# Split activations and split weights placed 32 bytes further into a 256-byte line, tile by tile

## The chip, the cores and the metric

The kernel runs on one core of a Trainium2 chip. Its time is device microseconds, the median of several runs. One execution is also recorded by the hardware profiler; times of single instructions come from that record.

## What is computed

A trunk of two layers on x, 512 tokens by 1024 features, in float32, with a norm behind it:

```
for i in range(DEPTH):                    # DEPTH = 2
    h = rmsnorm(x, norm_mix_g[i])
    h = chunked_spatial_gating(h, ...)    # layer 0: w_in [1024, 4096], w_out [2048, 1024]
    h = retention(h, ...)                 # layer 1 instead: w_in [1024, 6144], w_out [2048, 1024]
    x = x + h
    h = rmsnorm(x, norm_ffn_g[i])
    a = relu(h @ mlp_w1[i])               # [1024, 4096]
    x = x + (a * a) @ mlp_w2[i]           # [4096, 1024]
return rmsnorm(x, final_norm_g)
```

Nearly all of the arithmetic is in the products with the weight matrices.

## The kernel before, in words

**Three products for one.** A float32 product is made of float32r products, a faster and less exact form. Every operand is split into a high part (itself, rounded to float32r) and a low part (the rest). `mm3` (L207 to L210) adds high by high (L208), and the two mixed products (L209 and L210), into the same 128x512 block of PSUM; low by low is left out. A matmul here has 128x128 stationary weights, which PE loads ahead with an instruction of its own (PEld in the profile), and 512 moving columns.

**Activations.** The residual stream lies in xT: eight tiles xT0 to xT7 of 128 features by 512 tokens. `norm_split` (L219 to L223) makes of them hH0 to hH7 and hL0 to hL7, the split input of the products that follow a norm; these tiles are kept for the whole kernel. The results of the products lie in "big" tiles of 8192 bytes a partition, of which ten take turns: aH and aL (the squared activations of the dense layer), yH, yL, ryH and ryL (the mixers' gated results), q, k, v and others.

**Weights.** All matrices come in pieces of 1 MB by DMA into the tiles raw (two buffers of 8192 bytes). Each megabyte is two pieces. `prep` (L165 to L176) converts a piece into a tile wH (ScalarE, L172) and subtracts for wL (VectorE, L176); there are four buffers of wH and three of wL, of 4096 bytes each, taken in turn. `prep_tiles` (L160 to L163) takes the next buffers. The pieces have three shapes for three kinds of product, each with 1024 elements a partition: eight blocks of 128 columns, four of 256 or two of 512.

**Order.** The program is a list of steps written out by hand, each with one or two pieces of weights, and `refill` prepares the pieces ahead of the step that needs them. Evacuations and norms run behind later products. The names of products in the profile: v and u (gating's input), sg (its spatial mixing), o (its output); qk, vv and g (retention's input), sc and av (its scores and values), ro (its output); up and dn or dt (the two dense products, dt with tokens on the output's partitions, in the last layer). In v, u, qk, vv, g and up the activations are hH and hL; in o, ro, dn and dt they are slices of big tiles. In v, vv and dt the activations are the stationary operand and the weights the moving one, in the others it is the other way round.

**Where tiles lie.** Tiles are laid out in each partition in the order in which they are allocated, each rounded up to 32 bytes. The pool of kept tiles comes first: xT0 to xT7, hH0 to hH7, hL0 to hL7 (2048 bytes each), then ident, onesr and rows (512 each), gT (320), wide (4096), r4 and rh4 (16), vgh (64), rows2 (512), ssqv (64), rs4 (16), r2 (16), ssf (32) and ms0 (16), the last six at the places in the code where they are first needed. Behind it lie the weights' pool (two raw, four wH, three wL), the ten big tiles and the small working tiles. The first of the kept tiles begins 128 bytes into a 256-byte line.

Of the kernel before, what the change touches and what calls it, by code (L numbers as in the profile page):

```python
# [10 lines left out]
F32 = mybir.dt.float32  # L11
F32R = mybir.dt.float32r
# [5 lines left out]
P = 128  # L18
T = 512
D = 1024  # L20
KD = D // P
NT = T // P
# [10 lines left out]
class Raw:  # L33
    """A megabyte of a weight matrix as it lies in SBUF: [128, a, b]."""

# [4 lines left out]
class Piece:  # L40
    """Half of a Raw, split into two float32r parts."""

# [5 lines left out]
def pieces_f(w, rows, cols):  # L48
    """Stationary weights: pieces [128, 8 k, 128 columns]."""
    out = []  # L50
    for c in range(cols[0], cols[1], 256):
        raw = Raw(w[rows[0] : rows[1], c : c + 256].rearrange("(k p) n -> p k n", p=P))
        for i in range(2):
            out.append(Piece(raw, (slice(None), slice(None), slice(i * P, (i + 1) * P)), [P, 8, P]))
    return out


def pieces_t(w, rows, cols, parts=1):
    """Moving weights: pieces [128, 2 k, 512 columns]."""
    out = []  # L60
    for r in range(rows[0], rows[1], 512):
        raw = Raw(w[r : r + 512, cols[0] : cols[1]].rearrange("(k p) n -> p k n", p=P), parts)
        for i in range(2):
            out.append(Piece(raw, (slice(None), slice(2 * i, 2 * i + 2), slice(None)), [P, 2, 512]))
    return out


def pieces_o(w, rows, cols):
    """Stationary weights of 512 rows: pieces [128, 4 k, 256 columns]."""
    out = []  # L70
    for c in range(cols[0], cols[1], 512):
        raw = Raw(w[rows[0] : rows[1], c : c + 512].rearrange("(k p) n -> p k n", p=P))
        for i in range(2):
            out.append(Piece(raw, (slice(None), slice(None), slice(i * 256, (i + 1) * 256)), [P, 4, 256]))
    return out
# [3 lines left out]
def trunk(ctx, tc, x, norm_mix_g, norm_ffn_g, a_w_in, a_b_in, a_v_norm_g, a_w_s, a_b_s, a_w_out,  # L79
# [32 lines left out]

# [1 line left out]
    xT = [keep.tile([P, T], F32, name=f"xT{k}") for k in range(KD)]  # L114
    hH = [keep.tile([P, T], F32R, name=f"hH{k}") for k in range(KD)]
    hL = [keep.tile([P, T], F32R, name=f"hL{k}") for k in range(KD)]
    ident = keep.tile([P, P], F32, name="ident")
    onesr = keep.tile([P, P], F32R, name="onesr")
    rows = keep.tile([P, P], F32, name="rows")
    gT = keep.tile([P, 80], F32, name="gT")  # L120
    wide = keep.tile([P, D], F32, name="wide")
    rbc, r2bc = wide[:, 0:T], wide[:, T:D]
    r4 = keep.tile([P, NT], F32, name="r4")
    rh4 = keep.tile([P, NT], F32, name="rh4")
    vgh = keep.tile([P, 16], F32, name="vgh")
    make_identity(nc, ident)
    nc.gpsimd.memset(rows, 1.0)
# [7 lines left out]
    ]  # L135
    rows2 = keep.tile([16, P], F32, name="rows2")
    nc.scalar.dma_start(out=rows2, in_=vecs[0])
    nc.scalar.copy(out=onesr, in_=rows)
    MIX, FFN, VG, HG, BU = 0, 16, 32, 48, 64

# [1 line left out]
    order, steps, raws, pending = [], [], [], []  # L142
# [17 lines left out]
    def prep_tiles(i):  # L160
        p = order[i]
        p.hi = wts.tile(p.shape, F32R, tag="wH", name=f"wH{i}", bufs=4)
        p.lo = wts.tile(p.shape, F32R, tag="wL", name=f"wL{i}", bufs=3)  # L163

    def prep(upto, low=None):  # L165
        """Split the weights: the upper parts of all pieces before `upto`, the lower ones of those before `low`."""
        low = upto if low is None else low
# [38 lines left out]
    def mm3(ps, ah, al, bh, bl, start, stop):  # L206
        """ps += a.T @ b, of the parts' products all but the least."""  # L207
        nc.tensor.matmul(ps, lhsT=ah, rhs=bh, start=start, stop=False)  # L208
        nc.tensor.matmul(ps, lhsT=ah, rhs=bl, start=False, stop=False)  # L209
        nc.tensor.matmul(ps, lhsT=al, rhs=bh, start=False, stop=stop)  # L210

# [1 line left out]
    state = {}  # L213
# [5 lines left out]
    def norm_split(k, gcol):  # L219
        """h = x * g in two parts (the norm's scale comes in behind the product)."""  # L220
        g = gT[:, gcol + k : gcol + k + 1]
# [12 lines left out]
    def rsqrt(dst, a, n, name):  # L234
        """dst = a ** -0.5 on [128, n], by Newton's steps from the bits' half."""
        y, t = [work.tile([P, n], F32, tag=f"rs{i}_{n}", name=f"{name}_{i}", bufs=2) for i in range(2)]
# [22 lines left out]
    def stats(ssq, dst, scale, name):  # L259
        """dst[token, chunk] = rsqrt(mean of squares + eps)."""  # L260
        hi, lo = split(ssq, f"st_{name}", nc.gpsimd)
# [12 lines left out]
    def spread(src, dst, name):  # L274
        """dst[any partition, token] = src[token, chunk]."""
        d = []
# [10 lines left out]
    def norm(name, wide=True, square=False):  # L287
        """The statistics of the norm just summed, in steps behind work that doesn't need them."""
        yield from stats(state["ssq"], r4, 1.0 / D, name)
# [4 lines left out]

# [1 line left out]
    def mm_f(p, ps, bH, bL, ks, last):  # L296
# [8 lines left out]
    def feat(p, bufs, evac, name, behind=None):  # L305
        """One piece of stationary weights against all of b; behind() goes after the product."""
        def run(p):
# [9 lines left out]
    def feat_late(p, q, evacs, name):  # L317
        """Two pieces at once, each with the last k behind the others of both."""
        def run(p, q):
# [12 lines left out]
    def tokens(plist, bufs, evac, name, behind=None, last=None):  # L332
        """Pieces of moving weights: token-major results, four chunks at once."""
        accs = {}
# [29 lines left out]

# [1 line left out]
    win = a_w_in[0]  # L366
    v_raw, gu, yH, yL, bx = {}, {}, {}, {}, {}
    ssqv = keep.tile([P, NT, 4], F32, name="ssqv")
    rs4 = keep.tile([P, NT], F32, name="rs4")
    xr2 = [big([P, 2, NT, 256], F32, f"xr{b}") for b in range(2)]  # L370
# [33 lines left out]
    def ws_prep():  # L404
        """The gating weights, transposed to [s, t] with s <= t only."""
        w = bx["ws"]
# [11 lines left out]
    def gelu2(dst, z, z2):  # L418
        """dst = 2 gelu(z), with z's square in z2, in two steps."""
        nc.vector.scalar_tensor_tensor(out=z2, in0=z2, scalar=1.0 / GELU_K, in1=z, op0=ALU.add, op1=ALU.mult)  # L420
# [43 lines left out]
    def gate(f):  # L464
        """y chunk f = u * (spatially mixed v + bias), split."""
        j, c, g = f // 4, f % 4, f // 2
# [24 lines left out]
    def evac_x(gcol=None, scaled=False):  # L491
        """x += product; behind the last part of a sum, the next norm's chunk."""
        def ev(i, ps):
# [10 lines left out]
    def out_piece(p, i, h, name, gcol=None, before=None, behind=None):  # L504
        """x += w_out's rows of group h, two chunks of features."""
        ev = evac_x(gcol)
# [22 lines left out]
    def two_chunks(i):  # L529
        """The next piece, the next two chunks of x, and the squares of the last two."""  # L530
        prep(i + 2)
# [80 lines left out]

# [1 line left out]
    aH, aL = {}, {}  # L614
# [51 lines left out]

# [1 line left out]
    bw = b_w_in[0]  # L668
# [55 lines left out]
    def scores(h, j):  # L724
        """Decayed scores of keys in chunk j and all queries from there on, split."""
        if j == 0:
# [17 lines left out]
    def av(h, c):  # L744
        """Values' chunk c of the mixed head, with its squares, times gate and gain."""
        if c == 0:
# [91 lines left out]

# [1 line left out]
    xtok = [None, None]  # L840
    r2 = keep.tile([P, NT], F32, name="r2")
    ssf = keep.tile([P, NT, 2], F32, name="ssf")
    ms0 = keep.tile([P, NT], F32, name="ms0")

# [26 lines left out]
    def finish(n):  # L871
        """The last norm of token chunk n, a yield after every step. The Newton steps leave y scaled by
        -2 each, so that the bits' negative start ends at 8 / sqrt(a); the gain holds the eighth."""
        a = [work.tile([P, 1], F32, tag=f"fa{i}", name=f"fa{i}_{n}", bufs=2) for i in range(3)]
# [20 lines left out]
    def ends(bufs, accs, evac, *ps):  # L895
        """The last two pieces, the token chunks one after the other, each with its norm and way out."""
        aH, aL = bufs()
# [41 lines left out]

# [1 line left out]
    for h in range(2):  # L941
# [10 lines left out]
    load_a()  # L952
    # The array runs at half its clock until it has been busy for a while; the first loads are still under way.
    warm = mis("warm")
# [26 lines left out]
def _tables():  # L981
    """Rotary and decay tables: functions of the shapes alone."""
    f = np.float32
# [33 lines left out]
```

## Time and profile before

| | |
|---|---|
| Median of 3 runs | 1427.17 us |
| Lowest and highest run | 1425.28 and 1427.78 us |
| Span of the profiled execution | 1425.2 us |
| PE busy, matmuls recorded | 1410.2 us, 6290 |
| Weight loads busy | 1155.8 us |
| VectorE busy | 793.1 us (56%) |
| ScalarE busy | 507.0 us (36%) |
| GpSimd busy | 127.7 us (9%) |
| DMA | 135.23 MB, 95 GB/s on average |
| Mean granted TensorE clock | 0.998 |

The span runs from the first to the last instruction of the profiled execution. The profile gives no time of that execution besides the span; the span is 0.1 us below the fastest of the three runs. Durations of matmuls in the profile have a modelled end and overlap each other. The pace of PE is seen in the distance from one start to the next, in the timeline. A number such as L208 is the line of the kernel on which an instruction is issued.

### The profile page before, as it was taken

Reading aid. Unit: us, or ns where it says so; the run is one execution under the profiler, and the core shown is the slowest. Engines: PE = TensorE matmul, PEld = TensorE weight load, DVE = VectorE, ACT = ScalarE, POOL = GpSimd, SP = SyncE. Lnnn points to the kernel's source line nnn. Section 1 sums busy time; section 2 is a strip of 40 time slices with the busy share of each in tenths; the row PEclk is TensorE's granted clock in tenths of the full one; section 3 lists DMA queues with packets and bytes.
Section 4 is the critical chain, followed back from the end, with each engine's and each line's share of the span. In section 5 each row is a group of like instructions: output and inputs, shape, how many; then the busy total and the mean of one; then the engine's idle time right before and its main releaser. Section 6 shows DMA issues by size and latency. Waiting matters only on the chain.

```text
span 1425.2 us, 15372 instructions
## 1 busy us (share of the span) xinstructions
PE 1410.2 (99%) x6290; PEld 1155.8 (81%) x6290; DVE 793.1 (56%) x1102; ACT 507.0 (36%) x721; POOL 127.7 (9%) x98
## 2 busy tenths in 40 slices
PE   8999999999999999999999999999999999999997
PEld 7888888888888888888888878888888888888885
DVE  7757765775444444476646574564685443434435
ACT  4646633334313223123334333333334322313222
POOL 3010111220000000011111100110120000000002
PEclk9999999999999999999999999999999999999999
DMA  6332222232223322423222131132122332232221
GB/s 226 115 104 89 70 87 92 77 119 89 89 89 99 108 89 89 143 93 104 89 77 71 60 119 59 59 118 86 63 89 89 110 111 89 89 114 90 92 89 59
DMA packets 106101, 135.23 MB, mean 95 GB/s; under 512 B 2400, under 2 KB 79792, under 8 KB 105776
## 3 DMA queue, kind: packets, MB, share of 16 engines
q1 hardware_dynamic: 106000, 134.26, 28.8%
q8 instruction: 49, 0.80, 0.2%
q14 instruction: 20, 0.16, 0.0%
q10 hardware_dynamic: 32, 0.01, 0.0%
HBM read 132.16 MB, written 2.10 MB: 94 GB/s over the span
## 4 chain that ended last, share of the span: by engine, by line
PE 96%; DVE 3%; POOL 0%; ACT 0%; issue 0%; POOLq 0%; ACTq 0%; DVEq 0%
PE up L210 8%; PE up L208 8%; PE up L209 8%; PE dn L210 4%; PE dn L208 4%; PE dn L209 4%; PE dt L208 4%; PE dt L210 4%; PE dt L209 4%; PE g L208 2%; PE qk L208 2%; PE u L210 2%; PE u L209 2%; PE vv L208 2%; PE qk L210 2%; PE u L208 2%
## 5 line engine op out<-in xcount | busy, mean ns | idle before, releaser
L176 DVE TENSOR_TENSOR wL<-raw,wH 128x1024 fp32r<-128x1024 f32 x239 | 305.8, 1281 | 115.2 <-PE dt L209 65.6
L172 ACT CAST wH<-raw 128x1024 fp32r<-128x1024 f32 x239 | 249.5, 1044 | 265.8 <-PE dt L210 115.0
L208 PE MATMUL up<-hH,wH 128*128 128x512 f32 x480 | 189.9, 396 | 0.0
L210 PE MATMUL up<-hH,wL 128*128 128x512 f32 x480 | 189.5, 395 | 0.0
L209 PE MATMUL up<-hL,wH 128*128 128x512 f32 x480 | 189.5, 395 | 0.0
L626 DVE TENSOR_TENSOR aH<-r 128x512 fp32r<-128x512 f32 x64 | 45.0, 702 | 168.2 <-ACT r L624 168.1
L210 PEld LDWEIGHTS up<-hH,wL 128*128 128x128 f32 x480 | 90.2, 188 | 21.7
L208 PEld LDWEIGHTS up<-hH,wH 128*128 128x128 f32 x480 | 90.2, 188 | 21.5
L209 PEld LDWEIGHTS up<-hL,wH 128*128 128x128 f32 x480 | 90.2, 188 | 21.5
L209 PE MATMUL dt<-wL,aH 128*128 128x512 f32 x256 | 99.6, 389 | 0.0
L210 PE MATMUL dn<-aH,wL 128*128 128x512 f32 x256 | 99.6, 389 | 0.0
L209 PE MATMUL dn<-aL,wH 128*128 128x512 f32 x256 | 99.6, 389 | 0.0
L208 PE MATMUL dt<-wH,aH 128*128 128x512 f32 x256 | 99.6, 389 | 0.0
L208 PE MATMUL dn<-aH,wH 128*128 128x512 f32 x256 | 99.6, 389 | 0.0
L210 PE MATMUL dt<-wH,aL 128*128 128x512 f32 x256 | 99.6, 389 | 0.0
L624 ACT ACTIVATE r<-up 128x512 f32<-128x512 f32 x60 | 35.9, 598 | 174.8 <-PE up L210 174.8
L232 POOL TENSOR_TENSOR ssq<-ssq,sq 128x512 f32<-128x512 f32 x28 | 43.1, 1539 | 405.8 <-ACT sq L231 405.5
L496 DVE TENSOR_TENSOR xs<-dn,wide 128x512 f32<-128x512 f32 x32 | 22.1, 692 | 74.6 <-PE dn L210 74.6
L209 PEld LDWEIGHTS dn<-aL,wH 128*128 128x128 f32 x256 | 48.1, 188 | 10.1
L210 PEld LDWEIGHTS dt<-wH,aL 128*128 128x128 f32 x256 | 48.1, 188 | 10.0
L208 PEld LDWEIGHTS dt<-wH,aH 128*128 128x128 f32 x256 | 48.1, 188 | 10.0
L210 PEld LDWEIGHTS dn<-aH,wL 128*128 128x128 f32 x256 | 48.1, 188 | 10.0
(271 smaller groups left out, 2719.6 us busy)
## 6 DMA issues: line engine op xcount, KB each, us to landing
raw<-in_mlp_w_dram SPq DMA_DIRECT2D x64, 1024.0 KB, 5.1
raw<-in_b_w_in_dram SPq DMA_DIRECT2D x24, 1024.0 KB, 5.0
raw<-in_a_w_in_dram SPq DMA_DIRECT2D x14, 1024.0 KB, 5.1
raw<-in_a_w_out_dram SPq DMA_DIRECT2D x8, 1024.0 KB, 4.8
raw<-in_b_w_out_dram SPq DMA_DIRECT2D x8, 1024.0 KB, 5.0
raw<-in_a_w_in_dram SPq DMA_DIRECT2D x8, 256.0 KB, 6.2
out_dram<-out SPq DMA_DIRECT2D x8, 256.0 KB, 2.1
xr<-in_x_dram SPq DMA_DIRECT2D x3, 512.0 KB, 6.6
```

Source lines behind the costliest of these rows:

```text
L172: nc.scalar.copy(out=p.hi, in_=p.raw.tile[p.view])
L176: nc.vector.tensor_sub(out=p.lo, in0=p.raw.tile[p.view], in1=f32(p.hi))
L208: nc.tensor.matmul(ps, lhsT=ah, rhs=bh, start=start, stop=False)
L209: nc.tensor.matmul(ps, lhsT=ah, rhs=bl, start=False, stop=False)
L210: nc.tensor.matmul(ps, lhsT=al, rhs=bh, start=False, stop=stop)
L232: nc.gpsimd.tensor_tensor(out=state["ssq"], in0=state["ssq"], in1=sq, op=ALU.add)
L496: nc.vector.tensor_mul(t, ps, r2bc)
L624: nc.scalar.activation(r, ps, AF.Relu)
L626: nc.vector.tensor_mul(h, r, r)
```

## The change

It moves tiles; what is computed, and in which order, stays. The kept tiles are allocated in another order: the small ones first, then an unused tile of 1280 bytes, then xT, hH and hL. The tiles of hH and hL are 8 elements (32 bytes) longer than what is used of them, and so each begins 32 bytes further into a 256-byte line than the one before it: hH0 to hH7 and again hL0 to hL7 at 0, 32, ... 224 bytes. The buffers of wH and wL, too, have 8 elements more than the 1024 that are used; a view gives the used part the shape of the piece. The four wH buffers begin at 0, 32, 64 and 96 bytes into a line, the three wL buffers at 128, 160 and 192, and every big tile behind them at 224. xT and raw begin at 0. Comments and docstrings are removed as well, with the numbers of the lines kept up to the changed part.

```
-    xT = [keep.tile([P, T], F32, name=f"xT{k}") for k in range(KD)]
-    hH = [keep.tile([P, T], F32R, name=f"hH{k}") for k in range(KD)]
-    hL = [keep.tile([P, T], F32R, name=f"hL{k}") for k in range(KD)]
     ident = keep.tile([P, P], F32, name="ident")
     onesr = keep.tile([P, P], F32R, name="onesr")
     rows = keep.tile([P, P], F32, name="rows")
+    rows2 = keep.tile([16, P], F32, name="rows2")
...
     vgh = keep.tile([P, 16], F32, name="vgh")
+    ssqv = keep.tile([P, NT, 4], F32, name="ssqv")
+    rs4 = keep.tile([P, NT], F32, name="rs4")
+    r2 = keep.tile([P, NT], F32, name="r2")
+    ssf = keep.tile([P, NT, 2], F32, name="ssf")
+    ms0 = keep.tile([P, NT], F32, name="ms0")
+
+    keep.tile([P, 320], F32, name="fill")
+    xT = [keep.tile([P, T], F32, name=f"xT{k}") for k in range(KD)]
+    hH = [keep.tile([P, T + 8], F32R, name=f"hH{k}")[:, 0:T] for k in range(KD)]
+    hL = [keep.tile([P, T + 8], F32R, name=f"hL{k}")[:, 0:T] for k in range(KD)]
...
     def prep_tiles(i):
         p = order[i]
-        p.hi = wts.tile(p.shape, F32R, tag="wH", name=f"wH{i}", bufs=4)
-        p.lo = wts.tile(p.shape, F32R, tag="wL", name=f"wL{i}", bufs=3)
+        hi = wts.tile([P, 1024 + 8], F32R, tag="wH", name=f"wH{i}", bufs=4)
+        lo = wts.tile([P, 1024 + 8], F32R, tag="wL", name=f"wL{i}", bufs=3)
+        p.hi, p.lo = (t[:, 0:1024].rearrange("p (a b) -> p a b", a=p.shape[1]) for t in (hi, lo))
```

More of the change, by code (lines that the diff above doesn't have):

```diff
@@ L135, in trunk @@
     ]
-    rows2 = keep.tile([16, P], F32, name="rows2")
     nc.scalar.dma_start(out=rows2, in_=vecs[0])
@@ L367, in trunk @@
     v_raw, gu, yH, yL, bx = {}, {}, {}, {}, {}
-    ssqv = keep.tile([P, NT, 4], F32, name="ssqv")
-    rs4 = keep.tile([P, NT], F32, name="rs4")
     xr2 = [big([P, 2, NT, 256], F32, f"xr{b}") for b in range(2)]
@@ L840, in trunk @@
     xtok = [None, None]
-    r2 = keep.tile([P, NT], F32, name="r2")
-    ssf = keep.tile([P, NT, 2], F32, name="ssf")
-    ms0 = keep.tile([P, NT], F32, name="ms0")
     def to_tokens(c, n):
```

## The prediction

> **What bounds the kernel now.** I read the page first, then the waits of PE, then the groups of instructions with their forms kept apart, and last the timeline of PE alone in a few stretches.
>
> ```profile
> span 1425.2 us, 15372 instructions
> PE 1410.2 (99%) x6290; PEld 1155.8 (81%) x6290; DVE 793.1 (56%) x1102; ACT 507.0 (36%) x721; POOL 127.7 (9%) x98
> PEclk9999999999999999999999999999999999999999
> PE 96%; DVE 3%; POOL 0%; ACT 0%; issue 0%; POOLq 0%; ACTq 0%; DVEq 0%
> ```
>
> PE is busy for 99% of the span at the full granted clock, and the chain that ended last is PE's own for 96%. The waits of PE agree: the four that the profile lists sum to 4.6 us.
>
> ```profile
> PE xt L392 <- DVE wL L962: 1.4, 1, 1.4
> PE warm L956 <- POOL ident masks.py:199: 1.4, 1, 1.4
> PE bc_h L283 <- DVE dg_h L279: 0.9, 3, 0.3
> PE st_mix L265 <- POOL st_mix L256: 0.9, 1, 0.9
> ```
>
> So the time is the number of matmuls times their pace, and the only thing that this change can move is the pace. The groups:
>
> ```profile
> L208 PE MATMUL up<-hH,wH 128*128 128x512 f32 x480 | 189.9, 396 | 0.0
> L208 PE MATMUL u<-hH,wH 128*128 128x512 f32 x128 | 51.3, 401 | 0.0
> L208 PE MATMUL g<-hH,wH 128*128 128x512 f32 x128 | 51.1, 399 | 0.0
> L208 PE MATMUL qk<-hH,wH 128*128 128x512 f32 x128 | 50.7, 396 | 0.0
> L208 PE MATMUL vv<-wH,hH 128*128 128x512 f32 x128 | 50.6, 395 | 0.0
> L208 PE MATMUL v<-wH,hH 128*128 128x512 f32 x96 | 38.0, 396 | 0.0
> L557 PE MATMUL v<-wH,hL 128*128 128x512 f32 x32 | 8.7, 393 | 0.0
> L208 PE MATMUL up00a<-hH,wH 128*128 128x512 f32 x8 | 3.2, 395 | 0.0
> L208 PE MATMUL dn<-aH,wH 128*128 128x512 f32 x256 | 99.6, 389 | 0.0
> L208 PE MATMUL dt<-wH,aH 128*128 128x512 f32 x256 | 99.6, 389 | 0.0
> L209 PE MATMUL o<-yL,wH 128*128 128x512 f32 x128 | 49.9, 389 | 0.0
> L209 PE MATMUL ro<-ryL,wH 128*128 128x512 f32 x128 | 49.9, 389 | 0.0
> ```
>
> Of each name I show one of its three rows (the products high by high, high by low, low by high; all three have the same count; `up00a` stands for `up00a`, `up00b`, `up10a` and `up10b`). Every matmul with hH or hL in it, whether that is the moving or the stationary operand, has a mean of about 393 to 401 ns, and every one whose activations lie in a big tile (aH, aL, yH, ryL) has 389. The count of the first kind is 3 x (480 + 4 x 128 + 96 + 32) + 12 x 8 = 3456, of the second 3 x (256 + 256 + 128 + 128) = 2304. These durations overlap, since PE starts the next matmul before the modelled end of the last; the pace is read from starts. For each kind a long undisturbed stretch of PE's timeline, of which I show the first rows and the last:
>
> ```profile
> 448.62 0.39 PE L210 MATMUL up<-hH,wL 128*128 128x512 f32 x1
> 448.85 0.40 PE L208 MATMUL up<-hH,wH 128*128 128x512 f32 x1
> 449.09 0.39 PE L209 MATMUL up<-hL,wH 128*128 128x512 f32 x1
> 449.32 0.40 PE L210 MATMUL up<-hH,wL 128*128 128x512 f32 x1
> ...
> 469.62 0.39 PE L210 MATMUL up<-hH,wL 128*128 128x512 f32 x1
> ```
>
> ```profile
> 480.19 0.39 PE L208 MATMUL dn<-aH,wH 128*128 128x512 f32 x1
> 480.41 0.39 PE L209 MATMUL dn<-aL,wH 128*128 128x512 f32 x1
> ...
> 500.59 0.39 PE L208 MATMUL dn<-aH,wH 128*128 128x512 f32 x1
> ```
>
> `up` takes 21.00 us for 90 matmuls, 233.3 ns each, and it alternates between about 229 and 238. `dn` takes 20.40 us for 90, 226.7 ns each, all alike. Nothing waits in either stretch, and DVE and ACT come and go in both without a mark on the rhythm. What differs is where the activations lie. The sizes of the tiles, each rounded up to 32 bytes, give it: from hH0 to the first weight buffer lie 16 x 2048 bytes of hH and hL, then 6,784 bytes of small tiles, 39,552 in all, which is 154 lines of 256 bytes and a half. The weight buffers are 4096 and 8192 bytes, whole lines, so all weights and all big tiles begin at the same place of a line. The fast kind reads two operands from the same place of a line, the slow kind from places half a line apart.
>
> **The change part by part.** *No instruction, DMA or wait is added, removed or moved in order.* The fill is never written. The conversions and subtractions of the weights and of the norm write tiles that begin elsewhere. Were each a little slower, DVE with 44% of the span idle would hide it, and PE waits 4.6 us in all for other engines. The bound of that term is below 1 us.
>
> *What moves.* With the 32 bytes counted as places 0 to 7 of a line, from the first hH: hH k and hL k now lie at place k, the four wH buffers at 0 to 3, the three wL buffers at 4 to 6 and the big tiles, behind 7 x 32 more bytes, at 7. So the slow kind leaves its one relation (half a line) and passes through all eight from k to k. The fast kind leaves the same-place relation for good: 7 against 0 to 6. Both counts are at stake. Today they take 3456 x 233.0 = 805 us (233.0 lies between `up` and the 232.9 of `vv` below) and 2304 x 226.7 = 522 us, 1328 of the 1425 us, on average 230.5 ns each. The new time is the old one plus 5760 x (new pace - 230.5 ns). 1 ns is 5.8 us.
>
> *The price of a matmul in a new relation* is the unknown; the trace has only two of eight. From below it is bounded by columns alone, from two rows of one product with different widths:
>
> ```profile
> L208 PE MATMUL av<-pH,vvH 128*128 128x512 f32 x16 | 6.2, 390 | 0.0
> L208 PE MATMUL av<-pH,vvH 128*128 128x384 f32 x16 | 5.4, 336 | 0.0
> ```
>
> 54 ns for 128 columns are 0.42 ns a column, 2.4 columns a ns, so 512 columns are about 213 to 216 ns. Between 11 and 20 ns of every matmul are therefore not columns. From above it is bounded by the slower beat of `up`, 238 ns. The Trainium skill (TensorE: Matmul & The Clock Gate, Part 1, "Wait — 56ns, not 53.3ns?") gives N / 2.4 GHz and about 2.5 ns more for a warm matmul, 215.8 ns at 512 columns; by it the sum would be 5760 x -14.7 ns, some 85 us off. No row here with 512 columns comes near that.
>
> What are the 11 to 20 ns? In columns' time `dn` repeats after 544 = 34 x 16 and two of `up` after 1120 = 70 x 16. Here is `vv`, where hH is the stationary side:
>
> ```profile
> 664.32 0.40 PE L210 MATMUL vv<-wH,hL 128*128 128x512 f32 x1
> ...
> 665.95 0.40 PE L208 MATMUL vv<-wH,hH 128*128 128x512 f32 x1
> ```
>
> It repeats after seven matmuls, 1.63 us or 232.9 ns each; 244 x 16 columns' times would be 1.627 us. I read this as a slot that returns every 16 columns' times (6.7 ns): a read that comes at the wrong moment for its place in the line waits for its turn, and as every matmul begins at the same place again, each pays the rounding anew. `dn` shows a whole one, for a need that may lie anywhere over 528. If places differ from tile to tile, the turn comes earlier for some and later for others, and the rounding is paid in part: half of 6.7 ns off the best pace would be 223, and nothing off it 226.7. Against that stand the relations that are worse than the same place, up to the 233 of half a line; straight between 226.7 and 233.3, the mean over eight relations would be 230. I take 228.0 ns, between 223 and 233 and near 226.7, because that is the row nearest to a steady rhythm, and because from today's mean the trace leaves 15 ns below and only some 3 ns above. The sum: 5760 x (228.0 - 230.5) = -14.4 us. The span of 1425.2 us is just below the fastest of the runs shown (1425.28 to 1427.78), so I take the change off their median: 1427.2 - 14.4 = 1412.8 us.
>
> **The rivals.** *Slower: the change takes the good relation away from the fast kind.* This is where the trace has its one view of matmuls out of step, in `ro` behind the two `st` matmuls:
>
> ```profile
> 814.01 0.40 PE L208 MATMUL ro<-ryH,wH 128*128 128x512 f32 x1
> ...
> 816.10 0.39 PE L208 MATMUL ro<-ryH,wH 128*128 128x512 f32 x1
> ```
>
> Nine matmuls take 2.09 us, 232.2 ns each, though their operands lie at the same place of a line; then they fall back into 226.7. If a change of place from k to k throws every matmul out of step like this, the pace of all is about 232 ns: the slow kind gains 3456 x 0.8 = 2.8 us, the fast kind loses 2304 x 5.5 = 12.7 us, and the time is 1437. It decides from a mean pace of 230.5 ns on. For it speaks that `dn`, `dt`, `o` and `ro` have nothing to win by leaving the best pace seen; against it, that the disturbance there came from outside, by two matmuls of another kind, and was no regular step of 32 bytes.
>
> *No change: place doesn't matter.* The slow and the fast kind differ also in distance and in the tile that they come from, so the half line may be chance, and the change then moves nothing: 1427. The Trainium skill (same page, Part 2, "Step-by-step: what each phase is for") says that PE has two independent read ports into SBUF, one for the moving operand and one for the weights, so that loading weights takes nothing from a running matmul. By that rule the place of one operand could not matter to the other. The trace speaks against it, with 226.7 and 233.3 ns for the same shapes and engines' load. A second way to the same time is that gain and loss cancel: the slow kind at 229.8 ns and the fast kind at 231.5.
>
> *Much faster: the slots interleave.* If reads at different places never meet, the excess over columns mostly goes: at 220 ns the time would be 1427 - 60 = 1367. For it speaks that the excess exists in every row; against it, that in the rows above no two starts are closer than 0.22 us, in two relations and out of step.
>
> **How the numbers follow.** A measurement of this kernel tells about 0.2%, 2.9 us, from no change, which is 0.5 ns of pace. Likeliest is the middle case, with a pace between 225 and 230 (1395 to 1424): 0.45. Much faster, below 225: 0.08. No change, for either reason: 0.13. Slower: 0.34. Faster is thus 0.53. For 8 in 10 the range reaches from 223.9 ns, 38 us less, to 232.0 ns, 9 us more: 1389 to 1436. Both signs hold much of the chance; the likeliest case alone has 1395 to 1424.
>
> **What would show it.** Right: the groups of `up`, `u`, `g`, `qk` and `vv` fall by 3 to 6 ns a matmul, the alternation of 229 and 238 is gone from the timeline of `up`, and the starts there repeat with k, as eight relations follow each other; `dn` and `dt` stay within some 2 ns of 226.7; counts, waits and DVE's rows stay as they are. Wrong: `dn` and `dt` at 231 ns or more with `up` at 230 or more (the slower rival), the same two paces as now (place doesn't matter), or all near 216 to 220 (the slots interleave). PE's waits over 10 us, or rows of L172 or L176 longer by a tenth, would mean that a cost lies where I put none.

## The result and the profile after

The changed kernel takes 1435.31 us (median; 1433.39 to 1435.86) against 1427.11 us for the kernel before, a ratio of 1.0059 with a 95% interval from 1.0044 to 1.0073. It is slower by about 8 us. Its profiled execution, the fastest of its four runs, has a span of 1431.7 us, 6.5 us more than that of before.

The head of the page after, and its share of the chain of waits by engine:

```profile
span 1431.7 us, 15372 instructions
PE 1416.8 (99%) x6290; PEld 1154.2 (81%) x6290; DVE 794.8 (56%) x1102; ACT 506.3 (35%) x721; POOL 129.1 (9%) x98
...
PE 98%; DVE 1%; POOL 1%; ACT 0%; issue 0%; POOLq 0%; ACTq 0%; DVEq 0%
```

The count of instructions is the same to the last one, DVE and ACT are busy for the same time within 2 us, and PE alone is busy for 6.6 us more. PE's waits for others are these three, 4.3 us in all, where they were 4.6:

```profile
PE xt L398 <- DVE wL L965: 1.5, 1, 1.5
PE warm L959 <- POOL ident masks.py:199: 1.4, 1, 1.4
PE st_mix L273 <- POOL st_mix L264: 1.4, 1, 1.4
```

So it is the pace again. The groups by form (count, busy time, mean of one), of which I show one or two rows of a name:

```profile
L218 PE MATMUL up<-hH,wL 128*128 128x512 f32 x480 | 189.0, 394 | 0.0
...
L216 PE MATMUL dn<-aH,wH 128*128 128x512 f32 x256 | 101.2, 395 | 0.0
L216 PE MATMUL dt<-wH,aH 128*128 128x512 f32 x256 | 100.8, 394 | 0.0
...
L216 PE MATMUL o<-yH,wH 128*128 128x512 f32 x128 | 51.3, 400 | 0.0
...
L216 PE MATMUL g<-hH,wH 128*128 128x512 f32 x128 | 51.1, 399 | 0.0
...
L216 PE MATMUL vv<-wH,hH 128*128 128x512 f32 x128 | 50.6, 395 | 0.0
...
L217 PE MATMUL ro<-ryL,wH 128*128 128x512 f32 x128 | 50.4, 393 | 0.0
...
L217 PE MATMUL o<-yL,wH 128*128 128x512 f32 x128 | 50.3, 393 | 0.0
```

There is one kind left. Nearly all that read hH and hL is 0 to 2 ns better than before. Most of what read big tiles went from 389 to between 393 and 395; `o<-yH,wH`, already slower before, went from 394 to 400. The timeline says the same in starts. First and last of 90 matmuls of `up`, then of 84 of `dn`:

```profile
440.18 0.39 PE L216 MATMUL up<-hH,wH 128*128 128x512 f32 x1
...
461.05 0.39 PE L216 MATMUL up<-hH,wH 128*128 128x512 f32 x1
```

```profile
482.63 0.39 PE L216 MATMUL dn<-aH,wH 128*128 128x512 f32 x1
...
502.11 0.39 PE L216 MATMUL dn<-aH,wH 128*128 128x512 f32 x1
```

`up` needs 231.9 ns a matmul (233.3 before), `dn` 231.9 (226.7 before). Over the whole trace, the mean distance from the start of one of these matmuls to the next start (distances outside 205 to 255 ns left out) went from 232.9 to 231.9 ns for the slow kind and from 226.9 to 232.0 for the fast kind, together from 230.48 to 231.95. 1.47 ns times 5760 is 8.5 us, which is the loss.

### The profile page after: what moved, and what is told of

Same layout as the page of the kernel before. It is cut to its first block, busy times and chain, and to the rows that moved or that the text cites. A ratio compares the mean times of both kernels' runs of the same rounds, so it can differ in the third digit from the quotient of the medians.

```text
span 1431.7 us, 15372 instructions
## 1 busy us (share of the span) xinstructions
PE 1416.8 (99%) x6290; PEld 1154.2 (81%) x6290; DVE 794.8 (56%) x1102; ACT 506.3 (35%) x721; POOL 129.1 (9%) x98
## 4 chain that ended last, share of the span: by engine, by line
PE 98%; DVE 1%; POOL 1%; ACT 0%; issue 0%; POOLq 0%; ACTq 0%; DVEq 0%
PE up L216 8%; PE up L218 8%; PE up L217 8%; PE dn L216 4%; PE dn L217 4%; PE dn L218 4%; PE dt L216 4%; PE dt L218 4%; PE dt L217 4%; PE g L216 2%; PE ro L216 2%; PE qk L216 2%; PE o L216 2%; PE vv L216 2%; PE u L216 2%; PE ro L218 2%
## 5 line engine op out<-in xcount | busy, mean ns | idle before, releaser
L217 PEld LDWEIGHTS dt<-wL,aH 128*128 128x128 f32 x256 | 48.1, 188 | 11.2
```

## The experiments

The theory after the result: a matmul has the good pace only if its two operands lie at the same place of a 256-byte line; every other relation costs about the same, and the change gave the good one away. The rivals: a step of place from tile to tile is what costs, or place doesn't count at all. Places are in units of 32 bytes.

### All operands at one place

```
     hL = [keep.tile([P, T], F32R, name=f"hL{k}") for k in range(KD)]
+    keep.tile([P, 32], F32, name="fill")
```

> The kernel before with an unused tile of 128 bytes behind hL, so that weights, big tiles, hH and hL all begin at the same place of a line; no tile steps. Theory 1 (a matmul has the good pace of 226.7 ns only if its two operands lie at the same place of a line and stay there): the 3456 matmuls on hH and hL fall from about 233 to 226.7 ns and the rest keeps it, 3456 x 6.3 ns = 22 us off, about 1405 us, ratio 0.985. Theory 2 (the price is that of a step of place from tile to tile, and a steady relation of any size is cheap): the steady half line of the kernel before isn't what costs, about 1427 us. Theory 3 (it is the tile or its distance, not the place): 1427 us.

Measured: 1407.17 us (1406.67 to 1407.58) against 1426.9 us, ratio 0.9862 (0.9847 to 0.9877). An unused tile of 128 bytes saves 20 us. The groups of `up` and `vv`, and 90 matmuls of `up`:

```profile
L211 PE MATMUL up<-hH,wL 128*128 128x512 f32 x480 | 186.9, 389 | 0.0
...
L209 PE MATMUL vv<-wH,hH 128*128 128x512 f32 x128 | 49.9, 390 | 0.0
```

```profile
440.93 0.39 PE L209 MATMUL up<-hH,wH 128*128 128x512 f32 x1
...
461.33 0.39 PE L209 MATMUL up<-hH,wH 128*128 128x512 f32 x1
```

20.40 us for 90 are 226.7 ns: both kinds now have the pace that `dn` had. All tiles lie at another place of the line than `dn`'s did before (the weights moved by half a line, too), so it is the relation that counts and not the place itself. From hH0 to the first weight buffer are now 39,680 bytes, an odd number of 256-byte lines (155), while big tiles and weights lie an even number apart; both have the good pace, so the relation repeats after 256 bytes. The second and the third theory foretold 1427 us here, and fall.

### Each part of the change alone

The longer tiles of hH and hL in the kernel before (first), and the longer weight buffers in it (second, with the 128 bytes that put the first buffer at the place of hH):

```
-    hH = [keep.tile([P, T], F32R, name=f"hH{k}") for k in range(KD)]
+    hH = [keep.tile([P, T + 8], F32R, name=f"hH{k}")[:, 0:T] for k in range(KD)]
...
```

> The kernel before with the longer tiles of hH and hL alone, each 32 bytes further into a line than the one before; the weights and the big tiles stay at one place. Theory 1: the matmuls on hH and hL pass through all relations and take about 232 ns, some 1 ns less than before (3 us off), dn, dt, o and ro keep 226.7: about 1424 us. Theory 2: the step makes the matmuls on hH and hL no better or worse than 232 to 234: 1424 to 1431 us; the same for the rest. Theory 3: 1427 us.

```
-        p.hi = wts.tile(p.shape, F32R, tag="wH", name=f"wH{i}", bufs=4)
-        p.lo = wts.tile(p.shape, F32R, tag="wL", name=f"wL{i}", bufs=3)
+        hi = wts.tile([P, 1024 + 8], F32R, tag="wH", name=f"wH{i}", bufs=4)
+        lo = wts.tile([P, 1024 + 8], F32R, tag="wL", name=f"wL{i}", bufs=3)
+        p.hi, p.lo = (t[:, 0:1024].rearrange("p (a b) -> p a b", a=p.shape[1]) for t in (hi, lo))
```

> The kernel before with the longer buffers of the split weights alone (seven buffers at seven places, 32 bytes apart); hH and hL lie at one place, that of the first buffer, and the big tiles at one place, 7 x 32 bytes further. Theory 1: within a piece the high weights keep one relation and the low weights another, hardly ever the same place; dn, dt, o and ro go to about 232 ns (2304 x 5 ns = 12 us more), the matmuls on hH and hL stay at about 232: about 1437 us. Theory 2: places change only from wH to wL and back within a piece, so half of the price of the whole change: 1431 us. Theory 3: 1427 us.

Measured: with the activations' part alone 1425.87 us, ratio 0.9994 (0.9984 to 1.0003), no difference that can be told; with the weights' part alone 1434.59 us, ratio 1.0055 (1.0038 to 1.0072), the whole loss of the change. In the first, 90 matmuls of `up`; in the second, 90 of `dn`:

```profile
539.70 0.40 PE L209 MATMUL up<-hL,wH 128*128 128x512 f32 x1
...
560.62 0.40 PE L209 MATMUL up<-hL,wH 128*128 128x512 f32 x1
```

```profile
564.31 0.40 PE L210 MATMUL dn<-aH,wH 128*128 128x512 f32 x1
...
585.22 0.39 PE L210 MATMUL dn<-aH,wH 128*128 128x512 f32 x1
```

232.4 and 232.3 ns. The activations' part trades one bad relation for a mean over all (233.3 to 232.4 ns); the weights' part takes the good relation from `dn`, `dt`, `o` and `ro`. Theory 1 was out by about 2 us in each. The first run doesn't tell the theories apart, since all three foretold about its time; the second lies nearer to theory 1 (1437) than to theory 2 (1431).

### The other steady relations

Nothing steps in these three. The fill behind hL has 24, 8 and 48 elements, which puts hH and hL 1, 3 and 6 places ahead of the weights, and an unused tile at the head of the big tiles' pool puts those 2, 5 and 7 ahead:

```
+    bigp.tile([P, 16], F32, tag="pad", name="pad", bufs=1)
...
+    keep.tile([P, 24], F32, name="fill")
```

> No tile steps; hH and hL lie 1 place (32 bytes) ahead of the weights in a line, the big tiles 2 places. Theory 1: both kinds at about 230 to 233 ns, 1435 us in all. Theory 2: steady relations are cheap, both kinds at 227 or less, 1405 us or less. Theory 3: as before, 233 and 226.7 ns, 1427 us.

> No tile steps; hH and hL lie 3 places ahead of the weights in a line, the big tiles 5. Theory 1 in the form that only the same place is good: both kinds at 229 to 234 ns, about 1436 us. Rival: the price falls and rises with the offset, so that 3 costs more than 1 and 5 as much as 3: up to 1440 us, or some offset is better than the same place, with a pace below 226.7 ns and a time below 1407 us.

> No tile steps; hH and hL lie 6 places ahead of the weights, the big tiles 7. Theory 1 in the form that only the same place is good: both kinds at 229 to 234 ns, about 1436 us; an offset of 6 for moving activations is what 2 was for moving weights, 233 ns. Rival: some offset is better than the same place, below 226.7 ns and 1407 us.

Measured, one run each: 1436.21, 1444.54 and 1440.15 us, where the runs of before beside them gave 1426.9 us (median) and 1427.14 us. First and last of 90 matmuls, `up` and then `dn`, for offsets 1 and 2, 3 and 5, 6 and 7:

```profile
542.90 0.39 PE L212 MATMUL up<-hL,wH 128*128 128x512 f32 x1
...
563.90 0.39 PE L212 MATMUL up<-hL,wH 128*128 128x512 f32 x1
...
564.37 0.39 PE L211 MATMUL dn<-aH,wH 128*128 128x512 f32 x1
...
584.97 0.39 PE L211 MATMUL dn<-aH,wH 128*128 128x512 f32 x1
```

```profile
547.66 0.39 PE L212 MATMUL up<-hL,wH 128*128 128x512 f32 x1
...
568.66 0.39 PE L212 MATMUL up<-hL,wH 128*128 128x512 f32 x1
...
569.12 0.39 PE L211 MATMUL dn<-aH,wH 128*128 128x512 f32 x1
...
590.20 0.40 PE L211 MATMUL dn<-aH,wH 128*128 128x512 f32 x1
```

```profile
545.32 0.40 PE L212 MATMUL up<-hL,wH 128*128 128x512 f32 x1
...
566.32 0.40 PE L212 MATMUL up<-hL,wH 128*128 128x512 f32 x1
...
566.79 0.40 PE L211 MATMUL dn<-aH,wH 128*128 128x512 f32 x1
...
587.78 0.40 PE L211 MATMUL dn<-aH,wH 128*128 128x512 f32 x1
```

Worked out from these, and from the stretches shown above for 0 and 4:

| moving operand ahead of the weights by (places) | 0 | 1 | 2 | 3 | 4 | 5 | 6 | 7 |
|---|---|---|---|---|---|---|---|---|
| ns a matmul | 226.7 | 233.3 | 228.9 | 233.3 | 233.3 | 234.2 | 233.3 | 233.2 |

The sign counts. In `dt` the weights move, so the first of these three kernels has it at 6 places ahead and not at 2: its mean distance of starts is 233.3 ns, where `dn` has 228.9.

There is no slope: one relation is good, 2 is nearly as good, and the other six are about the price of half a line. No relation of the eight is better than the same place. The times follow: the mean distances of all these matmuls, 232.1, 233.6 and 232.8 ns, put into the prediction's sum, give 1436, 1445 and 1440 us. So theory 1 was right in the first run and too low by 8 and 4 us in the others, and a price that rises and falls with the offset is out.

The mean of the eight is 232.0 ns, that of the seven without the same place 232.8. Were the relation all that counts, these would be the paces of the slow and of the fast kind in the changed kernel; it has 231.9 and 232.0. Nothing is left there for the step of place itself.

### Whose weights must share the place?

hL and wL half a line behind hH and wH. PE loads the next product's weights while a product runs, so the moving operand could collide with its own weights' place or with those that are being loaded.

```
+    bigp.tile([P, 32], F32, tag="pad", name="pad", bufs=1)
...
+    keep.tile([P, 32], F32, name="fill")
     hL = [keep.tile([P, T], F32R, name=f"hL{k}") for k in range(KD)]
...
+        if i == 0:
+            wts.tile([P, 32], F32, tag="pad", name="padw", bufs=1)
         p.lo = wts.tile(p.shape, F32R, tag="wL", name=f"wL{i}", bufs=3)
```

> The kernel of same places, with hL and wL half a line (4 places) behind hH and wH; big tiles stay at the place of the high weights. This tells which weights the moving operand must share its place with. Rival a, those of its own product: in the matmuls on hH and hL two of three products have operands half a line apart, so 231 to 233 ns; about 1435 us with the other kind at 230. Rival b, those that PE loads meanwhile for the next product: hH runs while wH is loaded, hL while wL is loaded, hH while the next wH is loaded, always at the same place, though the place changes by half a line between them: 226.7 to 229 ns for v, u, qk, vv, g and up, some 230 for dn, dt, o and ro, about 1417 us.

Measured: 1432.09 us (one run), between the two. The three products of `dn`, in the order in which they run (wH with aH, wH with aL, wL with aH; only wL lies apart), and the first of `dt` (aH with wH as the moving side):

```profile
L213 PE MATMUL dn<-aH,wH 128*128 128x512 f32 x256 | 99.7, 389 | 0.0
L214 PE MATMUL dn<-aL,wH 128*128 128x512 f32 x256 | 101.4, 396 | 0.0
L215 PE MATMUL dn<-aH,wL 128*128 128x512 f32 x256 | 101.6, 397 | 0.0
...
L213 PE MATMUL dt<-wH,aH 128*128 128x512 f32 x256 | 101.7, 397 | 0.0
```

From their starts to the next start they take 226.9, 232.5, 234.1 and 235.7 ns on average. The first is good, by both rivals. The second has its own weights at the same place and is bad, for which, of the two, only the loading of wL beside it accounts. The third is bad as well, while wH is loaded at its place; its own weights lie apart. The loads alone don't explain `up` either: by rival b it would have 226.7 to 229 ns, and its mean is 231.1.

The row of `dt` fits neither rival: its own stationary tile and the one that is loaded beside it (aH again) lie at its place. What lies half a line away there is the moving operand of the next matmul, wL. So a change of the moving operand's place from one matmul to the next seems to cost as well; this is argued from one row. Which read waits for which stays open.

### Both operands stepping together

hH, hL and, inside their buffers, the weights of `up`, `u`, `g` and `qk` step by one place from k to k; the second kernel of the pair takes k from 7 down to 0 (and so sums in the other order).

```
+        if p.step:
+            p.hi, p.lo = (t.rearrange("p (a b) -> p a b", a=8)[:, :, 0:P] for t in (hi, lo))
+        else:
+            p.hi, p.lo = (t[:, 0:1024].rearrange("p (a b) -> p a b", a=p.shape[1]) for t in (hi, lo))
```

> The kernel of same places, with hH and hL stepping by one place from k to k, and the weights of up, u, g and qk stepping with them inside their buffer (8 unused elements behind each block of 128 columns). Weights and activations of a product so share their place, and it moves on by one place every three matmuls; v and vv, whose weights don't step, see all relations. If the relation is all that counts: up, u, g and qk stay at 226.7 to 227 ns, v and vv go to 232, about 1411 us. If a step of place costs by itself (the kernel falls out of step at each): up, u, g and qk at 229 to 232 ns, 1419 to 1425 us.

> As the kernel in which both operands step by k, but each product of up, u, g and qk takes its k from 7 down to 0, so that both operands step back by one place every three matmuls instead of on by one. If a slot that returns every 16 columns' times sets the starts, three matmuls took 3 x 256 + 63 pairs of columns there (692.5 ns), one less than a multiple of eight, because each place further on makes the turn come one pair earlier; back by one place they must take one more than a multiple of eight: 817 pairs (680.8 ns, 226.9 a matmul) or 825 (687.5 ns, 229.2 a matmul), 1408 to 1414 us in all. If any step of place costs by itself, whichever way: 230 to 232 ns as there, about 1420 us.

Measured: 1420.46 and 1421.3 us (one run each). 90 matmuls of `up` with the step on, and with the step back:

```profile
538.21 0.39 PE L216 MATMUL up<-hL,wH 128*128 128x512 f32 x1
...
558.93 0.39 PE L216 MATMUL up<-hL,wH 128*128 128x512 f32 x1
```

```profile
538.56 0.40 PE L216 MATMUL up<-hL,wH 128*128 128x512 f32 x1
...
559.33 0.40 PE L216 MATMUL up<-hL,wH 128*128 128x512 f32 x1
```

230.2 and 230.8 ns, where a product's operands always share their place. So the relation within a product isn't all: a step every third matmul costs some 4 ns on each, whichever way it goes. At each step the next weights lie a place apart from the moving operand. If weights that are being loaded cost what the table says, which isn't shown, that would be (2 x 226.7 + 233.3) / 3 = 228.9 ns, not 230.5, and would account for a little over half of it. The slot that I had read out of the rhythm gave 226.9 or 229.2 ns for the step back; it took 230.8, and that reading falls.

### Half a place

The weights 16 bytes further in, in the kernel of same places:

```
+        hi = wts.tile([P, 1088], F32R, tag="wH", name=f"wH{i}", bufs=4)
+        lo = wts.tile([P, 1088], F32R, tag="wL", name=f"wL{i}", bufs=3)
+        p.hi, p.lo = (t[:, 4:1028].rearrange("p (a b) -> p a b", a=p.shape[1]) for t in (hi, lo))
```

> The kernel of same places, with all split weights 16 bytes further in (an offset of half a place, the same for all buffers, nothing steps). If a place of 32 bytes is the unit and only the place in which an operand begins counts: 226.9 ns as with same places, 1407 us. If the offset counts in bytes, half a place costs like a whole one or in between: 229 to 233 ns for both kinds, 1420 to 1440 us.

Measured: 1420.69 us (one run). `dn` keeps its pace, `dt`, where the weights are the moving side, loses it, and `up` and `o` are in between:

```profile
L210 PE MATMUL up<-hH,wH 128*128 128x512 f32 x480 | 188.2, 392 | 0.0
...
L210 PE MATMUL dt<-wH,aH 128*128 128x512 f32 x256 | 100.9, 394 | 0.0
...
L210 PE MATMUL dn<-aH,wH 128*128 128x512 f32 x256 | 99.6, 389 | 0.0
...
L212 PE MATMUL o<-yH,wL 128*128 128x512 f32 x128 | 50.3, 393 | 0.0
```

`up` mixes two rhythms: one stretch of 90 matmuls from 534.23 us on takes 20.40 us, the good pace, others more. From start to start, the means are 226.7 ns for `dn`, 228.9 for `up`, 230.0 for `o` and 231.7 for `dt`. With the moving operand 16 bytes behind the weights (`dn`, `up` and `o`) the good rhythm is thus one of several; 16 bytes ahead (`dt`, `vv`) no stage keeps it. The offset counts in finer steps than 32 bytes.

## Why the prediction was wrong

**What bounds the kernel: right.** The time moved with PE's pace alone; counts, waits and the work of DVE and ACT stayed. The reading that the two kinds differ by half a line was right as well, and it was worth more than the whole change: 20 us for 128 bytes. The groups were a little less clean than I wrote: `o<-yH,wH` had 394 ns among the fast kind, and two rows of `v` on L557, 439 and 412 among the slow.

**The price of a matmul in a new relation: the step that failed.** I took 228.0 ns, "because that is the row nearest to a steady rhythm", and it is 231.9 (231.95 over the whole trace). Between two known relations I had laid a slope and then a gain on top, from a slot whose waits would be spread by different places. The six relations that the trace didn't show cost 233.3, 228.9, 233.3, 234.2, 233.3 and 233.2 ns: the same place is an exception and not the end of a scale. With the six at the price of the known bad one, the sum is 5760 x (232.5 - 230.5) = 12 us more, on the right side. The measured time lies just inside the end of the range, 1436, but that end came from the chance that I gave to the slower rival, not from my reasoning for 228.0.

**The gain for the slow kind: right in direction, mis-sized, and in part by luck.** `up` fell by 1.4 ns in the stretch shown, not by 3 to 6. By the table it falls because two of the eight relations it passes through are cheap, not because a rounding is paid in part. The alternation of 229 and 238 did go, as foretold, without a gain worth the name; the starts don't repeat with k after the change, as they do where hH and hL alone step.

**The fast kind: wrong.** I said that it leaves its relation "for good" and still let it stay within some 2 ns of 226.7. It lost 5.2, and the weights' part alone brings the whole loss.

**The rivals.** The slower one was right, with its price (232 ns) and time (1437 us), and the sign that I named for it came: `dn` and `dt` over 231 ns with `up` over 230. Its reason, that a change of place throws every matmul out of step, isn't needed: by the table the mean over relations already gives that pace. Where both operands step together, some 2 ns of the loss remain that the table doesn't explain. That place doesn't matter is refuted: by the Trainium skill (TensorE: Matmul & The Clock Gate, Part 2, "Step-by-step: what each phase is for") the loading of weights takes nothing from the running matmul, but the same matmuls took 226.7 and 233.3 ns with nothing but 128 bytes of fill between the kernels. Whether it is the load that takes something, no run here shows alone. Slots that interleave weren't found at any offset.

## What to carry to other kernels

When PE is busy for 99% of the span, read the pace from starts, group by tiles, and ask what the fast group shares; here it was that moving operand and weights begin at the same place of a 256-byte line. Keep every size in the pools a multiple of 256 bytes ahead of such tiles, or fill it up: the same place held steadily beat every spread tried here (226.7 against 230 to 232 ns). A wrong relation held steadily doesn't (233.3). Before a layout is spread, price each relation in a kernel that holds it fixed: here the changed kernel came out within 1 ns of the mean of its relations, and no change of place gained anything by itself.

## What the runs showed of the hardware that was not expected

- The price of a wrong relation is a level and not a slope: 233 to 234 ns for six of the eight offsets, 228.9 with the moving operand 64 bytes ahead of the weights (233.3 with it 64 bytes behind), 226.7 with both at the same place.
- Stepping both operands together costs about 4 ns a matmul (230.2 and 230.8 against 226.7 ns). The weights that are loaded for the next product would explain a little over half of that, if their place counts as the table says.
- With the moving operand 16 bytes behind the weights, several rhythms occur in the same kernel: 226.7 ns for `dn`, 228.9 for `up`, 230.0 for `o`. Why a relation settles into its rhythm wasn't found.
